# Up projection with both activation parts in one 512-column product, a shared pool of seven PSUM banks, chunked norm and block scan

## The chip, the cores and the metric

One core of a Trainium2 chip runs the program. The time is what the device reports for one execution, in microseconds (us). Engines are named as in the profile: PE (TensorE, matrix products) with PEld (its loads of the stationary operand), DVE (VectorE), ACT (ScalarE), POOL (GpSimd) and SP (the queue that issues the weight transfers).

## What is computed

Two layers of a hybrid backbone over 256 tokens of width 2048: 128 context tokens (g = 0) and 128 latent tokens (g = 1). Everything is fp32.

```python
h = modulate(x, shift1, scale1)                       # shift, scale, gate from silu(c) @ w_mod + b_mod
q, k, v, hq, hff, hfb, hi, hgt = split_in(h @ w_in)   # 2048 x 6656
att = rms_norm(attend(q, k, v, sink), attn_g)         # 8 heads
hg, s_f, s_b = hgrn_mixer(hq, hff, hfb, hi, hgt, ...) # 8 heads, forward and backward scan in chunks of 32
mix = concatenate([att, hg]) @ w_o
x = layer_norm(ALPHA * x + gate1 * mix)
ffn = square(relu(modulate(x, shift2, scale2) @ w_up)) @ w_down   # 2048 x 8192, 8192 x 2048
x = layer_norm(ALPHA * x + gate2 * ffn)
```

Within a scan of 128 tokens, a chunk's outputs take the chunk itself (`o_intra`), and the states left by the chunks before it, each decayed by the chunks between.

## The kernel before, in words

**Weights and their parts.** All weights are streamed once. An item of the main stream is a block of 512 x 512 weights: SP brings it as two raw tiles of 128 x 1024 (10 raw buffers), ACT rounds each to the high part `wh` (L1324, fp32r), and DVE takes the rest as the low part `wl` (L1325). There are four buffers for each of them, so two items. The activations are split the same way into `hh` and `hl` (`split_act`, L406). A product is then high x high + high x low + low x high: three fp32r matmuls where one would stand.

**Units.** A unit is one 512-wide output block: four items (`kg`), or fewer. In a T unit (q, hq, the two gates, and the up projection) the weight is the stationary operand: for each of 4 row blocks k and 4 column blocks m, `mm_tile` issues three matmuls of 256 columns (L436 `wh` with `hh`, L438 `wh` with `hl`, L439 `wl` with `hh`). In an N unit (k/v, hi, hgt, w_o, w_down) the activations are stationary and the weights stream, in matmuls of 512 columns (L448 to L450): rows k 0 and 1 for g = 0, then for g = 1, then rows 2 and 3 for both. Each unit accumulates in two PSUM banks of a pool of three (`accp`). When the last item is done, the unit's `done` function reads them: for the up projection `d_up` (ACT relu and square, L1214 and L1215, then `split_act` into `fh`/`fl`), for the down projection `d_down` (DVE, L1236 and L1240), for w_o `add_gated` (L887 to L892). In each of the two layers there are 16 up units, and 16 down units.

**Modulation.** Blocks of `w_mod` are dealt between the items at fixed rates (`RATE`, `PRATE`). Some go to PE (`Mod`, L203: 2-column weights at four places of the array, L223 for the first ones), the others to DVE, four multiply-adds of 128 x 1024 a block (`ModH.mac`, L266); most of those lie in the first layer's MLP.

**Tasks.** Attention, scans and norms run as generators that `pump` advances: up to two steps in the middle of an item and three at its end. Their PSUM tiles come from a pool of four banks (`sdp`, function `bank`). `scan_task` (L684; 8 a layer) computes the products within chunks (`pI`, L748), and then those across chunks into `pX` in three rounds (L777): all four heads' `kd` (128 columns) as weights, 32 columns of `qb` moving, with DVE scaling the earlier chunks between the rounds (L774), a masked copy (L794) and a last scaling (L801).

**Norms.** Both norms of a layer but the very last (`ln_last`) run as: statistics (`ln_stat`), centre and scale of eight 128 x 512 tiles on DVE (`ln_head`, L909), and `ln_mod`: per 512 features and token part four transposes on PE (L931), scale and shift (DVE L934, L936 for g = 0, ACT L940 for g = 1), and the split (L408, L409). `ln_out` then multiplies and adds the norm's gain and bias on POOL (L1002, L1003), for the residual. POOL also does part of the gated sums (L892 and L1224).

**Order.** DVE, ACT and PE instructions are ordered by a scheduler when the program is built; POOL and SP keep the order of the code. Each engine works through its own list.

## Time and profile before

| | |
|---|---|
| three runs | 2641.39, 2641.58, 2647.34 us; median 2641.58 |
| the profiled execution | 2641.68 us, of which the span from the first to the last instruction is 2639.9 |
| PE busy | 2536.6 us, 96% of the span |
| DVE, ACT, POOL busy | 1862.5, 1214.5, 230.9 us (71, 46, 9%) |
| transfers | 652.91 MB, 247 GB/s on average |
| granted TensorE clock, mean over the span | 0.988 |

A matmul's end in the profile is modelled, and matmuls overlap; what one costs in a stream is the distance from its start to the next one's. Idle time in brackets at a row's end is that of the engine just before it, with what ended it. "POOL" rows are rough.

### The profile page before, as it was taken

What the parts mean: (1) busy time and instruction counts of PE and PEld (TensorE: products, weight loads), DVE (VectorE), ACT (ScalarE), POOL (GpSimd) and SP (SyncE); (2) the same over time, 40 slices, a digit from 0 to 9 for tenths busy, and PEclk for the clock granted to TensorE, in tenths of its full rate; (3) what the DMA queues carried; (4) which work ended last, traced back from release to release, by engine and by line L of the source; (5) the groups of instructions that cost most, each with busy time, mean ns of one, the idle gap of its engine ahead of it and who ended that gap; (6) DMA issues with size and microseconds to landing.
All of it is one profiled execution on the core that took longest, in us unless ns stands there. A gap on an engine that the chain in (4) does not pass through costs nothing.

```text
span 2639.9 us, 41114 instructions
## 1 busy us (share of the span) xinstructions
PE 2536.6 (96%) x16276; PEld 2178.1 (83%) x16276; DVE 1862.5 (71%) x2290; ACT 1214.5 (46%) x1655; POOL 230.9 (9%) x266
## 2 busy tenths in 40 slices
PE   7999999998999999999999999999799999999996
PEld 4787777756988979979887989888798998998985
DVE  3455777658887777887778888877865565656656
ACT  3434554434444533534434656644454454443442
POOL 2000000014100000000014100001420000000003
PEclk9999999999999999999999999999899999999998
DMA  9889778868887878787879556566566666666663
GB/s 359 287 283 324 265 244 273 297 231 323 281 307 276 276 261 287 265 281 258 287 251 331 195 191 204 177 228 212 186 225 208 222 202 227 212 207 225 205 206 115
DMA packets 192369, 652.91 MB, mean 247 GB/s; under 512 B 22752, under 2 KB 25376, under 8 KB 192176
## 3 DMA queue, kind: packets, MB, share of 16 engines
q1 hardware_dynamic: 177680, 614.56, 68.0%
q0 software_dynamic: 11552, 33.04, 4.4%
q8 instruction: 127, 2.08, 0.3%
q10 hardware_dynamic: 2944, 2.69, 0.3%
q14 instruction: 66, 0.54, 0.1%
HBM read 643.32 MB, written 6.88 MB: 246 GB/s over the span
## 4 chain that ended last, share of the span: by engine, by line
PE 76%; DMA 10%; DVE 9%; issue 3%; ACT 1%; SPq 0%; POOL 0%; DVEq 0%; ACTq 0%; POOLq 0%
PE acc L436 12%; PE acc L439 12%; PE acc L438 12%; PE acc L448 11%; PE acc L449 11%; PE acc L450 11%; DMA raw<-in_w_mod_dram 6%; DVE wl L1325 3%; DVE ma L266 2%; PE psm L203 2%; PE pX L777 1%; DMA raw<-in_w_up_dram 1%; DMA raw<-in_w_in_dram 1%; PE psm L223 1%; DMA out_nsf_dram<-lf 1%
## 5 line engine op out<-in xcount | busy, mean ns | idle before, releaser
L1324 ACT CAST wh<-raw 128x1024 fp32r<-128x1024 f32 x784 | 821.8, 1049 | 1140.3 <-PE acc L450 489.0
L1325 DVE TENSOR_TENSOR wl<-raw,wh 128x1024 fp32r<-128x1024 f32 x784 | 971.2, 1246 | 433.3 <-ACT wh L1324 406.6
L436 PE MATMUL acc<-hh,wh 128*128 128x256 f32 x3072 | 875.9, 285 | 3.4 <-DVE q L599 1.9
L439 PE MATMUL acc<-hh,wl 128*128 128x256 f32 x3072 | 870.5, 284 | 7.9 <-DVE wl L1325 7.7
L438 PE MATMUL acc<-hl,wh 128*128 128x256 f32 x3072 | 869.7, 283 | 1.2 <-DVE hl L409 1.2
L436 PEld LDWEIGHTS acc<-hh,wh 128*128 128x128 f32 x3072 | 589.0, 192 | 39.2 <-issue 26.0
L439 PEld LDWEIGHTS acc<-hh,wl 128*128 128x128 f32 x3072 | 588.6, 192 | 11.2 <-DVE wl L1325 10.4
L438 PEld LDWEIGHTS acc<-hl,wh 128*128 128x128 f32 x3072 | 589.0, 192 | 2.9 <-DVE hl L409 2.2
L266 DVE SCALAR_TENSOR_TENSOR ma<-raw,stat,ma 128x1024 f32<-128x1024 f32 x300 | 388.5, 1313 | 113.4 <-DMA raw<-in_w_mod_dram 111.8
L448 PE MATMUL acc<-wh,fh 128*128 128x512 f32 x1024 | 401.8, 392 | 7.0 <-DVE Z L1236 6.8
L449 PE MATMUL acc<-wl,fh 128*128 128x512 f32 x1024 | 400.4, 391 | 0.4 <-DVE wl L1325 0.4
L450 PE MATMUL acc<-wh,fl 128*128 128x512 f32 x1024 | 399.7, 390 | 0.0
L448 PEld LDWEIGHTS acc<-wh,fh 128*128 128x128 f32 x1024 | 193.0, 188 | 57.8 <-DVE Z L1236 8.1
L449 PEld LDWEIGHTS acc<-wl,fh 128*128 128x128 f32 x1024 | 193.0, 188 | 40.8 <-DVE wl L1325 1.5
L450 PEld LDWEIGHTS acc<-wh,fl 128*128 128x128 f32 x1024 | 193.1, 189 | 40.4
L448 PE MATMUL acc<-wh,hh 128*128 128x512 f32 x320 | 129.5, 406 | 3.0 <-ACT hh L408 2.4
L449 PE MATMUL acc<-wl,hh 128*128 128x512 f32 x320 | 127.5, 398 | 0.3 <-DVE wl L1325 0.3
L450 PE MATMUL acc<-wh,hl 128*128 128x512 f32 x320 | 125.9, 394 | 1.9 <-DVE hl L409 1.9
L448 PE MATMUL acc<-wh,mxh 128*128 128x512 f32 x256 | 105.0, 411 | 5.9 <-DVE G L887 5.3
L876 POOL DMA_DIRECT2D G<-gr x48 | 26.3, 548 | 953.2 <-DVE Z L1241 408.9
L203 PE MATMUL psm<-raw,stat 128*2 128x512 f32 x640 | 96.6, 598 | 8.1 <-DMA raw<-in_w_mod_dram 8.1
L450 PE MATMUL acc<-wh,mxl 128*128 128x512 f32 x256 | 101.5, 398 | 0.0
(366 smaller groups left out, 2124.6 us busy)
## 6 DMA issues: line engine op xcount, KB each, us to landing
raw<-in_w_mod_dram SPq DMA_DIRECT2D x384, 512.0 KB
raw<-in_w_up_dram SPq DMA_DIRECT2D x256, 512.0 KB
raw<-in_w_down_dram SPq DMA_DIRECT2D x256, 512.0 KB
raw<-in_w_in_dram SPq DMA_DIRECT2D x208, 512.0 KB
raw<-in_w_o_dram SPq DMA_DIRECT2D x64, 512.0 KB
G<-gr POOLq DMA_DIRECT2D x48, 256.0 KB, 5.1
...
```

The source lines that it names most:

```text
L203: pe.matmul(self.ps[32 * j:32 * j + 2, :], lhsT=stat[:, k, :], rhs=raw[j // 2][:, 512 * (j % 2):512 * (j % 2) + 512], start=k == 0, stop=k ...
L223: pe.matmul(self.ps[32 * j:32 * j + 2, :], lhsT=stat[:, 4 * k + j, :], rhs=raw[j // 2][:, 512 * (j % 2):512 * (j % 2) + 512], start=k == 0 ...
L266: dve.scalar_tensor_tensor(self.acc[g], raw[h], c, self.acc[g], ALU.mult, ALU.add)
L436: pe.matmul(ps, lhsT=w0, rhs=hi[:, k], start=f and k == 0 and m % 2 == 0, stop=False, skip_group_check=True)
L438: pe.matmul(ps, lhsT=w0, rhs=lo[:, k], start=False, stop=False, skip_group_check=True)
L439: pe.matmul(ps, lhsT=w1, rhs=hi[:, k], start=False, stop=e and k == 3 and m % 2 == 1, skip_group_check=True)
L448: pe.matmul(ps, lhsT=hi[:, k, gs], rhs=wh[k], start=f and k == 0, stop=False)
L449: pe.matmul(ps, lhsT=hi[:, k, gs], rhs=wl[k], start=False, stop=False)
L450: pe.matmul(ps, lhsT=lo[:, k, gs], rhs=wh[k], start=False, stop=e and k == 3)
L777: pe.matmul(pX[:, 128 * m + 32 * c:128 * m + 32 * c + 32], lhsT=kd[:, 128 * m:128 * m + 128], rhs=qb[:, 128 * m + 32 * c:128 * m + 32 * c ...
L1324: act.copy(wh, r)
L1325: dve.tensor_tensor(wl, r, wh.bitcast(F32), ALU.subtract)
```

## The change

Six edits stand in the diff:

1. The parts of an activation that belong together lie side by side: a tile now holds two row blocks, each with 256 columns of the high part and then 256 of the low part. A new kind of unit, W, is used by the up projection: `w_tile` issues one 512-column matmul of `wh` with both parts, and one 256-column matmul of `wl` with the high part into the first half of the bank. A W unit accumulates in four banks; the second half of each holds `wh` x low alone, so `d_up` first copies it out (ACT, 128 x 256) and adds it to the first half (DVE, 128 x 256), four times a unit, and takes the relu from the sum.
2. The pools of three and four banks become one of seven.
3. In the last item of an N unit, g = 0 is finished before g = 1 begins.
4. The scan's products across chunks: two rounds of 32 x 32 (chunk 0 to 1, and 2 to 3), and one of 64 x 64, written to their own partitions of `pX`; three ACT copies take the place of the masked copy, and DVE's running products are merged.
5. The norm is centred and applied per 512 features, g = 1 first; g = 0 is scaled and shifted in four DVE instructions of 128 x 128; activation splits are in halves.
6. `ln_out`, and the sums in `add_gated` and `pre_sum`, go from POOL to DVE; `ln_out` waits 24 steps, and spreads its work.

```diff
-    accp = ctx.enter_context(tc.tile_pool(name="accp", bufs=3, space=PS))
     modp = ctx.enter_context(tc.tile_pool(name="modp", bufs=1, space=PS))
-    sdp = ctx.enter_context(tc.tile_pool(name="sdp", bufs=4, space=PS))
+    sdp = ctx.enter_context(tc.tile_pool(name="sdp", bufs=7, space=PS))
...
+        if un.kind == "N" and e:
+            for g in range(2):
+                if g == 1:
+                    between()
+                n_tile(un, g, range(4), hl, wh, wl, f, e)
+            return
...
+    def w_tile(un, m, ks, hl, wh, wl, f, e):
+
+        if f and ks[0] == 0:
+            un.ps[m] = bank("acc")
+        ps = un.ps[m]
+        for k in ks:
+            x = hl[k // 2][:, k % 2]
+            w0, w1 = (w[k][:, 128 * m:128 * m + 128] for w in (wh, wl))
+            pe.matmul(ps, lhsT=w0, rhs=x.rearrange("p a t -> p (a t)"), start=f and k == 0, stop=False,
+                      skip_group_check=True)
+            pe.matmul(ps[:, 0:256], lhsT=w1, rhs=x[:, 0], start=False, stop=e and k == 3, skip_group_check=True)
...
+        def across(ss, ts):
+            for m in range(4):
+                pe.matmul(pX[rows(ss), cols(m, ts)], lhsT=kd[:, cols(m, ss)], rhs=qb[:, cols(m, ts)],
+                          start=True, stop=True, tile_position=(0, 32 * ss.start))
+
+        across(one(c0), one(c1))
+        across(one(c2), one(c3))
...
-            for m in range(4):
-                pe.matmul(pX[:, 128 * m + 32 * c:128 * m + 32 * c + 32], lhsT=kd[:, 128 * m:128 * m + 128],
-                          rhs=qb[:, 128 * m + 32 * c:128 * m + 32 * c + 32], start=True, stop=True)
...
+        dve.tensor_tensor(kdv[:, :, c0], kdv[:, :, c0], dm[:, :, c1:c1 + 1].to_broadcast([128, 4, 32]), ALU.mult)
+        dve.tensor_tensor(qbv[:, :, c3], qbv[:, :, c3], dm[:, :, c2:c2 + 1].to_broadcast([128, 4, 32]), ALU.mult)
+        across(early, late)
+        yield
+        aTv = v3(aT, 4)
+        for ss, ts in ((one(c0), one(c1)), (one(c2), one(c3)), (early, late)):
+            act.copy(aTv[rows(ss), :, rows(ts)], v3(pX, 4)[rows(ss), :, rows(ts)])
...
-            (dve if n == 3 else pool).tensor_tensor(y, y, t, ALU.add)
+            dve.tensor_tensor(y, y, t, ALU.add)
...
+            for g in (1, 0):
+                y = yt[key, n, g]
+                dve.tensor_scalar(y, y, mr[g][0], mr[g][1], ALU.subtract, ALU.mult)
+            for g in (1, 0):
                 y = yt[key, n, g]
                 pt = bank("pt")
...
+                scale_shift(t, pt, A[:, fs], B[:, fs], g)
+                split_act(hl, 0, slice(128 * g, 128 * g + 128), v3(t, 4))
...
-                pool.tensor_tensor(y, y, gt, ALU.mult)
-                pool.tensor_tensor(y, y, bt, ALU.add)
+                dve.tensor_tensor(y, y, gt, ALU.mult)
+                dve.tensor_tensor(y, y, bt, ALU.add)
...
-                    r = u("t")
-                    act.activation(r, un.ps[b], AF.Relu)
+                    r, low = u("t"), u("e1")
+                    for j in range(2):
+                        ps, c = un.ps[2 * b + j], slice(256 * j, 256 * j + 256)
+                        act.copy(low[:, c], ps[:, 256:512])
+                        dve.tensor_tensor(r[:, c], ps[:, 0:256], low[:, c], ALU.add)
+                    act.activation(r, r, AF.Relu)
```

PE, in an up unit of the first layer, before: two row blocks k of one column block m.

```order
L436 MATMUL acc_6416<-hh_5697,wh_6395 128x256
L438 MATMUL acc_6416<-hl_5698,wh_6395 128x256
L439 MATMUL acc_6416<-hh_5697,wl_6396 128x256
L436 MATMUL acc_6416<-hh_5697,wh_6395 128x256
L438 MATMUL acc_6416<-hl_5698,wh_6395 128x256
L439 MATMUL acc_6416<-hh_5697,wl_6396 128x256
```

The same place in the changed program:

```order
L478 MATMUL acc_5819<-ha_5686,wh_5618 128x512
L480 MATMUL acc_5819<-ha_5686,wl_5619 128x256
L478 MATMUL acc_5819<-ha_5686,wh_5618 128x512
L480 MATMUL acc_5819<-ha_5686,wl_5619 128x256
L478 MATMUL acc_5824<-ha_5686,wh_5618 128x512
L480 MATMUL acc_5824<-ha_5686,wl_5619 128x256
```

The six matmuls became four (the last two rows begin the next bank), and the weight `wh` is loaded once where it was loaded twice (each matmul has a load of its own).

DVE, around the end of an up unit in the first layer, where `wl` is the next weights' low part, `ma` a modulation sum and `fl` the activation's low part; before:

```order
L1325 TENSOR_TENSOR wl_9680<-raw_9547,wh_9679 128x1024
L266 SCALAR_TENSOR_TENSOR ma_9071<-raw_9689,stat,ma_9071 128x1024
L409 TENSOR_TENSOR fl_9668<-t_9669,fh_9667 128x512
L1325 TENSOR_TENSOR wl_9684<-raw_9549,wh_9683 128x1024
L409 TENSOR_TENSOR fl_9668<-t_9674,fh_9667 128x512
L266 SCALAR_TENSOR_TENSOR ma_9072<-raw_9689,stat,ma_9072 128x1024
L1325 TENSOR_TENSOR wl_9760<-raw_9603,wh_9759 128x1024
L1325 TENSOR_TENSOR wl_9764<-raw_9605,wh_9763 128x1024
```

The same place in the changed program (`t` is the sum of both halves of a bank):

```order
L265 SCALAR_TENSOR_TENSOR ma_8700<-raw_9264,stat,ma_8700 128x1024
L1353 TENSOR_TENSOR wl_9257<-raw_9146,wh_9256 128x1024
L1242 TENSOR_TENSOR t_9236<-acc_9050,e_1705_9237 128x256
L1242 TENSOR_TENSOR t_9236<-acc_9055,e_1705_9237 128x256
L1242 TENSOR_TENSOR t_9246<-acc_9060,e_1707_9247 128x256
L265 SCALAR_TENSOR_TENSOR ma_8701<-raw_9264,stat,ma_8701 128x1024
L1242 TENSOR_TENSOR t_9246<-acc_9065,e_1707_9247 128x256
L1353 TENSOR_TENSOR wl_9261<-raw_9148,wh_9260 128x1024
L413 TENSOR_TENSOR fa_9234<-t_9236,fa_9234 128x2x256
L265 SCALAR_TENSOR_TENSOR ma_8700<-raw_9266,stat,ma_8700 128x1024
L1353 TENSOR_TENSOR wl_9323<-raw_9186,wh_9322 128x1024
L413 TENSOR_TENSOR fb_9235<-t_9246,fb_9235 128x2x256
```

Four instructions of 128 x 256 stand ahead of the activation's split, among the same work.

PE, at the first norm of the second layer, from the last matmul of w_o on, before (`pt` are the transposes; one row further down stands last):

```order
L450 MATMUL acc_17832<-wh_17817,mxl_17388 128x512
L931 MATMUL pt_17921<-ident_597,Y_17008 128x128 x4
L931 MATMUL pt_17931<-ident_597,Y_17012 128x128 x4
L931 MATMUL pt_17945<-ident_597,Y_17135 128x128 x4
L931 MATMUL pt_17955<-ident_597,Y_17139 128x128 x4
L931 MATMUL pt_17969<-ident_597,Y_17253 128x128 x4
L931 MATMUL pt_17979<-ident_597,Y_17257 128x128 x4
L931 MATMUL pt_17993<-ident_597,Y_17442 128x128 x4
L436 MATMUL acc_18035<-hh_17919,wh_17851 128x256
L436 MATMUL acc_18048<-hh_17919,wh_17851 128x256
L438 MATMUL acc_18035<-hl_17920,wh_17851 128x256
...
L931 MATMUL pt_18003<-ident_597,Y_17446 128x128 x4
```

The same place in the changed program:

```order
L468 MATMUL acc_17077<-wh_17062,mxb_16625 128x512
L967 MATMUL pt_17160<-ident_592,Y_16249 128x128 x4
L967 MATMUL pt_17174<-ident_592,Y_16245 128x128 x4
L967 MATMUL pt_17192<-ident_592,Y_16376 128x128 x4
L967 MATMUL pt_17206<-ident_592,Y_16372 128x128 x4
L967 MATMUL pt_17224<-ident_592,Y_16494 128x128 x4
L967 MATMUL pt_17238<-ident_592,Y_16490 128x128 x4
L967 MATMUL pt_17256<-ident_592,Y_16685 128x128 x4
L967 MATMUL pt_17270<-ident_592,Y_16681 128x128 x4
L478 MATMUL acc_17296<-ha_17156,wh_17096 128x512
L480 MATMUL acc_17296<-ha_17156,wl_17097 128x256
```

Before, the eighth transpose stood a dozen matmuls behind the start of the up projection; now all eight stand ahead of its first matmul.

## Rows read from the trace of the kernel before

**Rows 1.** The page: busy time of each engine, and the chain that ended last by engine.
```profile
PE 2536.6 (96%) x16276; PEld 2178.1 (83%) x16276; DVE 1862.5 (71%) x2290; ACT 1214.5 (46%) x1655; POOL 230.9 (9%) x266
...
PE 76%; DMA 10%; DVE 9%; issue 3%; ACT 1%; SPq 0%; POOL 0%; DVEq 0%; ACTq 0%; POOLq 0%
```

**Rows 2.** Busy time by stretch: PE, PEld, DVE, ACT, POOL; then clock, DMA share, GB/s.
```profile
640.00:1390.00 750.00, 738.20 (x4697) 651.63 (x4697) 598.22 (x549) 336.18 (x372) 39.13 (x35) 1.00 0.81 276
...
1900.00:2618.00 718.00, 716.40 (x4599) 654.00 (x4597) 439.31 (x395) 326.92 (x366) 45.09 (x47) 1.00 0.63 207
```

**Rows 3.** Timeline of PE: start, duration; first and last of 22 matmuls of 256 columns.
```profile
1499.77 0.28 PE L436 MATMUL acc<-hh,wh 128*128 128x256 f32 x1
...
1502.29 0.28 PE L436 MATMUL acc<-hh,wh 128*128 128x256 f32 x1
```

**Rows 4.** Timeline of PE: first and last of 37 matmuls of 512 columns.
```profile
2609.64 0.39 PE L450 MATMUL acc<-wh,fl 128*128 128x512 f32 x1
...
2617.80 0.39 PE L450 MATMUL acc<-wh,fl 128*128 128x512 f32 x1
```

**Rows 5.** Groups by line on PEld: count, busy us, mean ns | idle before.
```profile
L777 PEld LDWEIGHTS pX<-t,ed 128*128 128x128 f32 x192 | 23.6, 192 | 0.6
...
L203 PEld LDWEIGHTS psm<-raw,stat 128*2 128x2 f32 x640 | 11.2, 82 | 42.4 <-issue 20.0 <-DMA raw<-in_w_mod_dram 18.3 <-DVE w L279 0.4
...
L275 PEld LDWEIGHTS ph<-ma,ones 128*32 128x32 f32 x80 | 1.6, 108 | 2.4 <-issue 1.7
```

**Rows 6.** Timeline of PEld: eight loads of one round across chunks.
```profile
1503.19 0.97 PEld L777 LDWEIGHTS pX<-t,ed 128*128 128x128 f32 x8
```

**Rows 7.** Waits of PE for an accumulating bank: us in total, times, longest.
```profile
PE acc L448 <- DVE Z L1236: 6.8, 3, 2.4
...
PE acc L448 <- DVE G L887: 5.3, 2, 3.5
```

**Rows 8.** Timeline at one of these waits, on PE and on DVE.
```profile
939.83 0.50 PE L448 MATMUL acc<-wh,fh 128*128 128x512 f32 x1 [2.23 <-DVE Z L1236]
...
939.10 1.28 DVE L1236 TENSOR_TENSOR Z<-Z,acc 128x512 f32<-128x512 f32 x2
```

**Rows 9.** Busy time by stretch, columns as in rows 2, behind each of the five waits.
```profile
596.00:600.00 4.00, 4.00 (x14) 3.23 (x13) 3.09 (x5) 1.05 (x1) 3.18 (x4) 0.57 0.87 297
940.00:945.00 5.00, 5.00 (x16) 3.93 (x17) 2.74 (x3) 1.04 (x1) 0.00 (x0) 0.66 0.99 354
991.00:996.00 5.00, 5.00 (x17) 3.91 (x16) 4.72 (x5) 1.04 (x1) 0.00 (x0) 0.66 0.91 281
1133.00:1138.00 5.00, 2.78 (x13) 1.98 (x12) 4.19 (x5) 0.82 (x2) 2.26 (x2) 1.00 0.93 301
1868.00:1873.00 5.00, 4.33 (x12) 3.46 (x13) 4.19 (x7) 1.04 (x1) 3.54 (x4) 0.66 0.82 270
```

**Rows 10.** Timeline at the first norm of the second layer, on PE and on DVE.
```profile
1879.73 0.39 PE L450 MATMUL acc<-wh,mxl 128*128 128x512 f32 x1
1886.94 3.29 PE L931 MATMUL pt<-ident,Y 128*128 128x128 f32 x16 [6.83 <-DVE Y L909]
...
1895.97 0.75 PE L436 MATMUL acc<-hh,wh 128*128 128x256 f32 x2
...
1879.66 1.28 DVE L887 TENSOR_TENSOR G<-acc,G 128x512 f32<-128x512 f32 x2
...
1886.25 6.60 DVE L909 TENSOR_SCALAR Y<-Y,s,s 128x512 f32<-128x512 f32 x8
```

**Rows 11.** Groups by line on DVE, 640 to 1390 us.
```profile
L1325 DVE TENSOR_TENSOR wl<-raw,wh 128x1024 fp32r<-128x1024 f32 x254 | 312.3, 1241 | 59.8 <-ACT wh L1324 56.2 <-DMA raw<-in_w_up_dram 1.7 <-DMA raw<-in_w_mod_dram 1.5
L266 DVE SCALAR_TENSOR_TENSOR ma<-raw,stat,ma 128x1024 f32<-128x1024 f32 x202 | 258.9, 1300 | 78.4 <-DMA raw<-in_w_mod_dram 77.0 <-ACT ma L264 1.2
```

**Rows 12.** Groups by line on ACT and on DVE, the whole span.
```profile
L824 ACT COPY lf<-pK 128x256 f32<-128x256 f32 x16 | 6.0, 377 | 5.0 <-PE pK L815 5.0
...
L854 DVE TENSOR_TENSOR Z<-Z,Z 128x256 f32<-128x256 f32 x8 | 3.0, 419 | 0.0
```

More of the change, by code (lines that the diff above doesn't have):

```diff
@@ L152, in derive_constants @@
     def derive_constants():
[L153 removed]
+        for key in ("fi", "bi"):
             r = up.tile([128, 128], I32, tag="w", name=nm("m" + key), bufs=BUFS["w"])
@@ new lines, in mm_tile @@
+            if un.kind == "N":
+                for g in range(2):
+                    n_tile(un, g, ks, hl, wh, wl, f, e)
+                continue
+            for m in range(4):
+                if un.kind == "W":
+                    w_tile(un, m, ks, hl, wh, wl, f, e)
+                    continue
+                if f and kk == 0 and m % 2 == 0:
+                    un.ps[m // 2] = bank("acc")
+                ps = un.ps[m // 2][:, 256 * (m % 2):256 * (m % 2) + 256]
+                for k in ks:
+                    w0 = wh[k][:, 128 * m:128 * m + 128]
+                    w1 = wl[k][:, 128 * m:128 * m + 128]
+                    x = hl[k // 2][:, k % 2]
+                    pe.matmul(ps, lhsT=w0, rhs=x[:, 0], start=f and k == 0 and m % 2 == 0, stop=False,
+                              skip_group_check=True)
+                    pe.matmul(ps, lhsT=w0, rhs=x[:, 1], start=False, stop=False, skip_group_check=True)
+                    pe.matmul(ps, lhsT=w1, rhs=x[:, 0], start=False, stop=e and k == 3 and m % 2 == 1,
+                              skip_group_check=True)
@@ new lines, in n_tile @@
+    def n_tile(un, g, ks, hl, wh, wl, f, e):
+        if f and ks[0] == 0:
+            un.ps[g] = bank("acc")
+        ps = un.ps[g]
+        gs = slice(128 * g, 128 * g + 128)
+        for k in ks:
+            hi, lo = (hl[k // 2][:, k % 2, i, gs] for i in range(2))
+            pe.matmul(ps, lhsT=hi, rhs=wh[k], start=f and k == 0, stop=False)
+            pe.matmul(ps, lhsT=hi, rhs=wl[k], start=False, stop=False)
+            pe.matmul(ps, lhsT=lo, rhs=wh[k], start=False, stop=e and k == 3)
@@ new lines, in scan_task @@
+        early, late = slice(min(c0, c1), max(c0, c1) + 1), slice(min(c2, c3), max(c2, c3) + 1)
+        cols = lambda m, sl: slice(128 * m + 32 * sl.start, 128 * m + 32 * sl.stop)
+        rows = lambda sl: slice(32 * sl.start, 32 * sl.stop)
+        one = lambda c: slice(c, c + 1)
+        pX = bank("pX")
+        def across(ss, ts):
+            for m in range(4):
+                pe.matmul(pX[rows(ss), cols(m, ts)], lhsT=kd[:, cols(m, ss)], rhs=qb[:, cols(m, ts)],
+                          start=True, stop=True, tile_position=(0, 32 * ss.start))
@@ new lines, in scan_task @@
+        across(one(c0), one(c1))
+        across(one(c2), one(c3))
+        qS = lf[:, 256:512]
+        cum = small(8).rearrange("p (h c) -> p h c", h=2)
+        do = dm[:, 1::2]
+        dve.memset(cum[:, :, c0:c0 + 1], 1.0)
+        for x in range(1, 4):
+            pc, cc = order[x - 1], order[x]
+            dve.tensor_tensor(cum[:, :, cc:cc + 1], cum[:, :, pc:pc + 1], do[:, :, pc:pc + 1], ALU.mult)
+        for hl in range(2):
+            dve.tensor_tensor(qS[:, 128 * hl:128 * hl + 128].rearrange("p (c t) -> p c t", c=4),
+                              qbv[:, 2 * hl + 1], cum[:, hl, :].unsqueeze(2).to_broadcast([128, 4, 32]), ALU.mult)
@@ L920, in ln_coef, with scale_shift @@
         return A, B
+    def scale_shift(out, src, A, B, g):
+        for c in range(4):
+            o_, s_ = (x[:, 128 * c:128 * c + 128] for x in (out, src))
+            if g == 0:
+                dve.tensor_scalar(o_, s_, A[:, c, g:g + 1], B[:, c, g:g + 1], ALU.mult, ALU.add)
+            else:
+                act.activation(o_, s_, AF.Identity, scale=A[:, c, g:g + 1], bias=B[:, c, g:g + 1])
     def ln_mod(key, AB, dst):
         A, B = AB
+        mr = ln_stat(key)
         for n in range(4):
             hl = new_act("h")
-            for g in range(2):
+            fs = slice(4 * n, 4 * n + 4)
+            for g in (1, 0):
+                y = yt[key, n, g]
+                dve.tensor_scalar(y, y, mr[g][0], mr[g][1], ALU.subtract, ALU.mult)
+            for g in (1, 0):
                 y = yt[key, n, g]
```

148 lines of the change are left out of this document (41 added, 107 removed).

## The prediction

> **What bounds the kernel now.** I read the page's busy shares first: PE is busy for 96% of the span and holds 76% of the chain that ended last; DVE is at 71%, ACT at 46% [rows 1]. A busy PE need not be a working one, so the table by stretches comes next: in both MLPs PE is busy almost throughout, with a clock of 1.00, while the transfers have room (DMA share 0.81 and 0.63) [rows 2]. In the timeline of PE the matmuls then follow each other evenly: 21 steps from the first 256-column matmul to the last of 22 take 2.52 us, 120 ns each [rows 3], and 36 steps of 512 columns take 8.16 us, 227 ns each [rows 4]. So the end is set by the number and width of matmuls, plus the places where PE stands still. Changes to DVE, ACT and POOL count only where PE waits for them.
>
> The sum is made against the profiled execution: 2641.7 us with a span of 2639.9 and 1.8 around it; the median of the three runs is 2641.6, so no correction follows. A measurement of this kernel can tell about 0.3%, 8 us, from no change.
>
> **The up projection.** There are 32 up units of 4 items, each with 4 row blocks and 4 column blocks: 2048 places where three 256-column matmuls become one of 512 and one of 256. Twice 120 ns is 240, and the wide one takes 227: each place falls from 360 to 347 ns. 2048 x 13.3 ns = **27 us** saved, all on the path. The columns stay the same; what goes is the fixed part of one matmul, since a matmul's second 256 columns cost 227 - 120 = 107 ns, and its first 256 cost 120: 13 ns stand there whatever the width. Two pages differ here: the Trainium skill ("TensorE: Matmul & The Clock Gate", section "Back-to-back issue gap") gives a warm isolated matmul N/2.4 + 2.5 ns, a fixed part of 2.5 ns, by which the edit would be worth 5 us (an estimate from that page: 2048 x 2.5 ns). The rows show 13 ns in a dense stream, and the measurement decides; the rule stays as a rival.
>
> **The scan across chunks.** Before, a scan issues 24 matmuls on PE (4 heads, 3 rounds, and two instructions for each fp32 product: 384 loads over 16 scans, 192 in each of two groups like the one shown [rows 5]). Their loads start (0.97 - 0.19) / 7 = 111 ns apart [rows 6]; 16 x 24 x 111 ns = 43 us. They are bound by the load of 128 columns, not by the 32 columns that move. Loads last 192 ns for 128 columns, 108 for 32, 82 for 2 [rows 5]: 0.87 ns a column on top of some 80 that overlap. After, a scan has 16 with 32-column and 8 with 64-column weights: 28 and 56 ns by that slope, 0.9 us a scan, 14 us in all. That is 28 us less; at the old distance it would be nothing. I take **22 us**, nearer to the slope, since it gives the 111 ns of 128 columns right, and leave some for the changes between small and full products. DVE's and ACT's part of the scan lies beside PE.
>
> **The banks.** PE waits five times for the DVE that empties an accumulating bank: 6.8 us behind L1236 and 5.3 behind L887 [rows 7, 8]. Behind four of them the granted clock is 0.57 or 0.66 over 4 to 5 us [rows 9], that is 1.2 GHz for a part of it: 4 x 0.43 and three times 5 x 0.34, 6.8 us more. Together 19 us. With seven banks an N unit (two banks) finds free ones although the two before are not emptied. But W units take four: where one W unit follows another (24 places) the fourth bank of the next needs the first bank of the last. I take **14 us** saved; the ends are 0 and 19.
>
> **New work on DVE and ACT.** Each up unit gets four ACT copies (0.38 us) and four DVE additions (0.42 us) of 128 x 256 [rows 12]. ACT is at 45% in the first MLP [rows 2]. DVE had 598 of 750 us there [rows 2]; it gets 64 x 0.42 = 27 us, and 16 instructions of `ln_out` and 8 of `pre_sum` at 0.64 us (the pair of L887 takes 1.28 [rows 10]), 15 us: 640 of 736, 87% instead of 80%. What covers it is DVE's idle time: 56 us waiting for ACT's casts, 77 for modulation weights [rows 11]. Where that is gone, `wl` comes late, and PE waits. I put **4 us** on it; ends 0 and 14 (the whole gain of that layer's up units). In the second MLP DVE has 439 of 718 us [rows 2]: nothing.
>
> **The norms.** At the first norm of the second layer PE does not work on weights from 1879.73 to 1895.97 [rows 10]. The earlier finish of g = 0 brings DVE's chain forward by about one instruction of 0.64 us. Against it, all eight transposes now stand ahead of the up projection, and the last one waits for a centre instruction that has 12 scalings of 128 x 128 and 12 half splits ahead of it on DVE: 8 x 0.82 us (6.60 for eight) [rows 10], 12 x 0.42 [rows 12], and 12 at half of that, 14 us after 1886.25, or 1899 to 1900; without the slow centre pace (0.5 each) 1897. So this norm loses 1 to 4 us, and the other norms and the tail win the 0.64 us each. Net **+1 us**; ends -4 and +6.
>
> **ln_out later.** In the second layer's input projection the `Z` buffers are held until `ln_out` has stored them; ACT's two copies of the first gate unit then stand ten casts apart, and hold a bank. **+2 us**; ends 0 and 10 (two waits of the size in rows 7, with the slow clock behind).
>
> Sum: -27 - 22 - 14 + 4 + 1 + 2 = -56; 2641.7 - 56 = **2586 us**.
>
> **The rivals.**
> - *DVE sets the pace of the first MLP.* For: 87% in an ordered queue, with modulation sums that wait for transfers. Against: 133 us of its idle time stood in waits that a later DVE shortens. Price: that layer's 13.6 us and as much as 5 more: about 2604.
> - *The small matmuls across chunks keep 111 ns.* For: no matmul with 32-column weights and few moving columns stands in the trace. Against: loads shorten with their columns [rows 5]. 2586 + 22 = 2608.
> - *The wide matmul saves little,* because the fixed part belongs to something else than the count, so that 512 + 256 columns take some 358 ns. 2048 x 11 ns: 2608. Against: both distances are even over dozens of matmuls [rows 3, 4]. (This is what the page's 2.5 ns would mean.)
> - *Slower: W waits for its fourth bank.* The next W unit needs it three column blocks (6 matmul pairs of a half item, 2.08 us) after its start, and the bank got its last matmul as long before the end: DVE and ACT have 4.2 us. At rows 8 DVE released a bank when it had been done for 3.9 us (its last g = 0 matmul ended near 935.9, PE went on at 939.8). If that lag were the rule and two more us, a wait of 2.2 us and 1.7 of slow clock at 24 places cost 94 us: 2680. It decides from a lag of 4.2 us on, and turns the sign from about 2.3 us lost at each place. Against: three such lags in the first layer, none in the second.
> - *Everything comes at its good end*: -27 - 28 - 19 - 4 = -78: 2564.
>
> **How the numbers follow.** Chances: forecast 0.64 (2572 to 2598), DVE 0.13, small matmuls 0.07, wide matmul 0.02, all good 0.08, slower 0.06. The range of 8 in 10 runs from 2562 to 2613: it takes in all but the last, and leaves out two faults at once. Faster by over 0.3% (below 2633.7): 0.92; within: 0.02, taken from the forecast's share for two of the faults at once, with a little of the fourth rival; slower: 0.06, that rival beyond its point.
>
> **What would show it.** In the changed profile: pairs of 512 and 256 columns 347 ns apart in the up projection; the group of `pX` at about 14 us from start to start; no wait of the matmuls of N units for L1265 or L916 (the lines of L1236 and L887 there); DVE near 640 us in the first MLP, with `wl` waits of PE under 5 us; weights taken up again at the second layer's first norm some 16 to 20 us after the last matmul of w_o. The prediction is wrong if PE waits for `acc` at the start of W units, if DVE's idle time in the first MLP goes to nothing, or if the pairs are slower than 350 ns.

## The result, and the profile after

The changed kernel took 2600.05 us (median of four runs, 2598.75 to 2603.59), the kernel before 2641.48 beside it: 0.984 of the time, 95% interval 0.9823 to 0.9857, or 41 us less. The prediction was 2586 us with a range of 2562 to 2613: the time lies in it, and the sign is right. But 56 us were forecast, and the 15 that are missing are not one small thing: two terms were mis-sized by 12 and 6 us, and a gain that carries much of the result stood nowhere in the sum.

The profiled execution has a span of 2599.2 us (2639.9 before). Cut at the starts of the first and last matmul of each stage's weights, in us (a norm is the stretch between the last matmul of one stage and the first of the next):

| stage | before | after | difference |
|---|---|---|---|
| up to the first weights | 34.3 | 33.1 | -1.2 |
| layer 0: input projection, attention, scans, w_o | 574.0 | 564.0 | -10.0 |
| norm a | 15.1 | 17.9 | +2.8 |
| layer 0: MLP | 767.7 | 744.2 | -23.5 |
| norm b | 14.7 | 16.9 | +2.2 |
| layer 1: input projection to w_o | 473.9 | 465.8 | -8.1 |
| norm c | 16.2 | 19.0 | +2.8 |
| layer 1: MLP | 721.8 | 717.5 | -4.3 |
| tail | 22.1 | 20.8 | -1.3 |

The line of busy times, which answers to [rows 1], shows what still bounds the kernel: PE, at 96% of a shorter span. POOL lost more than half of its work.

```profile
PE 2502.0 (96%) x14228; PEld 2051.9 (79%) x14228; DVE 1895.1 (73%) x2500; ACT 1268.3 (49%) x1871; POOL 105.0 (4%) x188
```

The table by stretches (columns as in [rows 2]): both MLPs, and two stretches behind a wait of PE for a bank. DVE has 606 of 719 us in the first MLP, 84%, so it did not become the bound; in the last two rows the clock is 0.79, a part at 1.2 GHz.

```profile
640.00:1359.00 719.00, 713.18 (x3627) 585.60 (x3626) 606.46 (x619) 348.45 (x428) 11.93 (x23) 1.00 0.81 282
...
1861.00:2578.00 717.00, 714.26 (x3599) 604.01 (x3599) 461.67 (x484) 344.97 (x429) 15.64 (x30) 1.00 0.62 208
...
1218.00:1226.00 8.00, 5.92 (x27) 4.55 (x30) 7.99 (x11) 3.98 (x7) 0.00 (x0) 0.79 0.75 246
1886.00:1894.00 8.00, 5.26 (x21) 4.24 (x21) 6.49 (x9) 4.50 (x8) 0.00 (x0) 0.79 0.55 178
```

The timeline of PE in the second MLP answers to [rows 3, 4]. From the first 512-column matmul to the last one there are 14 pairs in 4.95 us: 353.6 ns a pair, where 347 were forecast.

```profile
2100.16 0.40 PE L478 MATMUL acc<-ha,wh 128*128 128x512 f32 x1
2100.39 0.28 PE L480 MATMUL acc<-ha,wl 128*128 128x256 f32 x1
...
2105.11 0.40 PE L478 MATMUL acc<-hb,wh 128*128 128x512 f32 x1
```

Averaged over the 1,985 pairs of the trace that no wait and no half clock interrupts it is 352.4: 235.5 from the wide to the narrow one and 116.9 back. The steps are uneven: in long stretches two pairs take 349 or 350 ns and the third 360 or 361. The place with three 256-column matmuls took 359.7 before, so the pair saves 7.3 ns.

What PE waits for from 33 us on, by line (us in total, times, longest); of [rows 7] nothing is left, neither L1265 nor L916 appears. In their place stand the sums of W units (L1242), the centring (L962) and the modulation copies (L229, 0.7 us in the kernel before).

```profile
PE pI L778 <- DVE e L772: 13.3, 6, 4.2
PE pt L967 <- DVE Y L962: 12.3, 3, 6.5
PE acc L478 <- DVE t L1242: 6.9, 4, 2.7
PE pt L232 <- ACT w L229: 5.6, 6, 1.9
```

The loads of the products across chunks, by line and shape (count, busy us, mean ns), answer to [rows 5]: 137 ns for 64 columns and 112 for 32, where 128 columns took 192.

```profile
L801 PEld LDWEIGHTS pX<-ed,t 128*64 128x64 f32 x64 | 4.3, 137 | 5.2 <-DVE ed L818 3.5 <-DVE wl L1353 0.7 <-DVE s L812 0.4
...
L801 PEld LDWEIGHTS pX<-t,ed 128*32 128x32 f32 x128 | 4.1, 112 | 3.0 <-issue 1.5 <-PE acc L456 0.3 <-PE acc L468 0.3
```

From start to start all matmuls of `pX` take 19.5 us, 40.0 before.

Norm c, on PE and on DVE, answers to [rows 10]. The first six centrings take 0.47 us each (0.82 before, as a mean over two kinds: see e7); then scalings and splits follow, and the last centring starts 11.3 us after the first. PE stands for it from the 24th transpose on.

```profile
1841.83 0.39 PE L468 MATMUL acc<-wh,mxb 128*128 128x512 f32 x1
1848.73 4.89 PE L967 MATMUL pt<-ident,Y 128*128 128x128 f32 x24 [6.50 <-DVE Y L962]
1859.22 1.97 PE L967 MATMUL pt<-ident,Y 128*128 128x128 f32 x8 [5.59 <-DVE Y L962]
1860.84 0.78 PE L478 MATMUL acc<-ha,wh 128*128 128x512 f32 x1
...
1848.13 2.83 DVE L962 TENSOR_SCALAR Y<-Y,s,s 128x512 f32<-128x512 f32 x6
1850.87 1.04 DVE L949 TENSOR_SCALAR ed<-pt,A,B 128x128 f32<-128x128 f32 x3
...
1859.41 0.55 DVE L962 TENSOR_SCALAR Y<-Y,s,s 128x512 f32<-128x512 f32 x1
```

DVE in the first MLP, around the wait at 1007 us: a multiply-add stands 4.3 us for its modulation weights at the head of the list, and the low part and three sums of a W unit, which have all they need, stand behind it.

```profile
1000.96 1.23 DVE L1353 TENSOR_TENSOR wl<-raw,wh 128x1024 fp32r<-128x1024 f32 x1 [0.65 <-ACT wh L1352]
1006.48 1.28 DVE L265 SCALAR_TENSOR_TENSOR ma<-raw,stat,ma 128x1024 f32<-128x1024 f32 x1 [4.30 <-DMA raw<-in_w_mod_dram]
1007.68 1.22 DVE L1353 TENSOR_TENSOR wl<-raw,wh 128x1024 fp32r<-128x1024 f32 x1
1008.82 1.08 DVE L1242 TENSOR_TENSOR t<-acc,e 128x256 f32<-128x256 f32 x3
```

### The profile page after: what moved, and what is told of

It is laid out like the page before. It is cut to its first block, busy times and chain, and to the rows that moved or that the text cites. A ratio compares the mean times of both kernels' runs of the same rounds, so it can differ in the third digit from the quotient of the medians.

```text
span 2599.2 us, 37416 instructions
## 1 busy us (share of the span) xinstructions
PE 2502.0 (96%) x14228; PEld 2051.9 (79%) x14228; DVE 1895.1 (73%) x2500; ACT 1268.3 (49%) x1871; POOL 105.0 (4%) x188
## 4 chain that ended last, share of the span: by engine, by line
PE 57%; issue 33%; DMA 5%; DVE 3%; ACT 2%; POOL 1%; SPq 0%; POOLq 0%; DVEq 0%; ACTq 0%
PE acc L478 11%; PE acc L466 8%; PE acc L468 8%; PE acc L467 8%; PE acc L480 6%; PE acc L453 3%; PE acc L455 3%; PE acc L456 3%; DMA raw<-in_w_mod_dram 2%; PE psm L202 2%; PE psm L222 1%; DMA raw<-in_w_in_dram 1%; DVE wl L1353 1%; PE pI L778 1%; DMA G<-in_lnb_dram 1%
## 5 line engine op out<-in xcount | busy, mean ns | idle before, releaser
L478 PE MATMUL acc<-ha,wh 128*128 128x512 f32 x1024 | 370.5, 401 | 6.9 <-DVE t L1242 6.9
L478 PE MATMUL acc<-hb,wh 128*128 128x512 f32 x1024 | 370.0, 401 | 0.0
L480 PE MATMUL acc<-hb,wl 128*128 128x256 f32 x1024 | 289.2, 282 | 0.0
L480 PE MATMUL acc<-ha,wl 128*128 128x256 f32 x1024 | 288.6, 282 | 0.1
L467 PE MATMUL acc<-wl,fb 128*128 128x512 f32 x512 | 199.5, 390 | 1.6 <-DVE wl L1353 1.6
L466 PE MATMUL acc<-wh,fa 128*128 128x512 f32 x512 | 200.5, 392 | 0.0
L466 PE MATMUL acc<-wh,fb 128*128 128x512 f32 x512 | 199.9, 390 | 0.0
L467 PE MATMUL acc<-wl,fa 128*128 128x512 f32 x512 | 199.5, 390 | 0.0
L468 PE MATMUL acc<-wh,fb 128*128 128x512 f32 x512 | 199.4, 390 | 0.0
L468 PE MATMUL acc<-wh,fa 128*128 128x512 f32 x512 | 199.4, 389 | 0.0
L453 PE MATMUL acc<-ha,wh 128*128 128x256 f32 x512 | 149.4, 292 | 0.0
L453 PE MATMUL acc<-hb,wh 128*128 128x256 f32 x512 | 147.6, 288 | 0.0
L455 PE MATMUL acc<-hb,wh 128*128 128x256 f32 x512 | 146.1, 285 | 0.0
L455 PE MATMUL acc<-ha,wh 128*128 128x256 f32 x512 | 145.8, 285 | 0.0
L456 PE MATMUL acc<-hb,wl 128*128 128x256 f32 x512 | 145.5, 284 | 0.0
```

Source lines behind the costliest of these rows:

```text
L453: pe.matmul(ps, lhsT=w0, rhs=x[:, 0], start=f and k == 0 and m % 2 == 0, stop=False, skip_group_check=True)
L455: pe.matmul(ps, lhsT=w0, rhs=x[:, 1], start=False, stop=False, skip_group_check=True)
L456: pe.matmul(ps, lhsT=w1, rhs=x[:, 0], start=False, stop=e and k == 3 and m % 2 == 1, skip_group_check=True)
L466: pe.matmul(ps, lhsT=hi, rhs=wh[k], start=f and k == 0, stop=False)
L467: pe.matmul(ps, lhsT=hi, rhs=wl[k], start=False, stop=False)
L468: pe.matmul(ps, lhsT=lo, rhs=wh[k], start=False, stop=e and k == 3)
```

## The experiments

Twelve kernels, in three groups of four; each group ran on one chip beside the kernel before, whose median was 2642.63, 2648.69 and 2644.97 us there. So groups are compared by their ratio to it, and 0.001 is 2.6 us. Stage times are those of the profiled execution, cut as in the table above; one execution can lie some us from the median, and where that matters it is said.

### Why a pair takes 353 ns: e1, e2, e3 and e12

In e1 the second matmul of a pair gets 512 columns as well:

```diff
-            pe.matmul(ps[:, 0:256], lhsT=w1, rhs=x[:, 0], start=False, ...)
+            pe.matmul(ps, lhsT=w1, rhs=x.rearrange("p a t -> p (a t)"), start=False, ...)
```

> The changed kernel, with the second matmul of every pair in a W unit widened to 512 columns too (low part of the weight times both parts of the activation, which adds the product low x low that the reference kernel leaves out). A pair of 512 and 256 columns takes 353.4 us/1000 = 353.4 ns on average in the changed kernel, and not 346.7 (120 + 226.7). Theory A, alternating widths cost it: a stream of 512 columns alone runs at 226.7 ns, a pair at 453, 2048 x 100 ns = +204 us, 2804 us. Theory B, the form of W units costs it (every matmul brings other weights than the one before, the activation's two parts are read as one row): some 230 ns each, a pair at 460, +218 us, 2818 us.

2805.81 us (one run). On the timeline of PE, 24 matmuls lie between the two rows: 5.44 us, 227 ns each.

```profile
2030.25 0.39 PE L478 MATMUL acc<-hb,wh 128*128 128x512 f32 x1
...
2035.69 0.39 PE L478 MATMUL acc<-ha,wh 128*128 128x512 f32 x1
```

Averaged, a pair takes 453.6. So a W unit's form costs nothing: other weights for every matmul, activation parts read as one row and four banks run at the 227 ns of [rows 4]. What costs 5.7 ns a pair (352.4 against 120 + 226.7) is that 512 and 256 columns stand in one stream.

In e2 the order within a column block is 512, 512, 256, 256:

```diff
         for k in ks:
             x = hl[k // 2][:, k % 2]
...
-            pe.matmul(ps[:, 0:256], lhsT=w1, rhs=x[:, 0], start=False, ...)
+        for k in ks:
+            x = hl[k // 2][:, k % 2]
+            pe.matmul(ps[:, 0:256], lhsT=wl[k][:, 128 * m:128 * m + 128], rhs=x[:, 0], start=False, ...)
```

> The changed kernel, with the two rows of a W unit's column block in the order 512, 512, 256, 256 instead of 512, 256, 512, 256: same matmuls, half as many changes of width. Theory A (a change of width costs some 3.4 ns): two pairs take 700 instead of 707 ns, 1024 x 6.7 ns = 7 us less, 2593 us. Theory B (the form of W units): no change of the distances, 2600 us but for waits for the low part, which is needed 227 ns later: at most 2 us less.

2590.56 us, 0.9801 (0.9784 to 0.9818). Rows of PE, two matmuls each; 12 pairs from the first to the last row in 4.18 us, 348.3 ns a pair:

```profile
2100.33 0.63 PE L477 MATMUL acc<-ha,wh 128*128 128x512 f32 x2
2100.79 0.40 PE L481 MATMUL acc<-ha,wl 128*128 128x256 f32 x2
...
2104.51 0.63 PE L477 MATMUL acc<-hb,wh 128*128 128x512 f32 x2
```

As expected of theory A, and about 10 us less for a swap of two lines: averaged, a pair takes 348.3 ns, and 2048 x 4.1 ns are 8.4.

e12 went on: two column blocks together, four matmuls of 512 and then four of 256 (on top of e11, below).

```diff
+                for m in (0, 2):
+                    w_tile(un, (m, m + 1), ks, hl, wh, wl, f, e)
...
+        for m in ms:
...
+            for k in ks:
+                x = hl[k // 2][:, k % 2]
+                pe.matmul(un.ps[m], lhsT=wh[k][:, 128 * m:128 * m + 128], ...
...
+        for m in ms:
+            for k in ks:
+                x = hl[k // 2][:, k % 2]
+                pe.matmul(un.ps[m][:, 0:256], lhsT=wl[k][:, 128 * m:128 * m + 128], rhs=x[:, 0], start=False, ...
```

> The kernel of e11, with two column blocks of a W unit together: four matmuls of 512 columns, then four of 256. A quarter of the changes of width of the changed kernel instead of half: 3.4 ns a pair less if a change of width costs 3.4 ns, divided by two for the half that is left, 512 x 6.7 ns = 3.5 us less than e11. Rival: the fourth bank is needed 0.47 us earlier, and waits come back: no gain.

2587.29 us, 0.9781 (0.9759 to 0.9803), where e11 has 0.9763: no gain, and not for want of banks. The pairs themselves are slower, 12 in 4.21 us or 351 ns:

```profile
2100.55 1.09 PE L477 MATMUL acc<-hb,wh 128*128 128x512 f32 x4
...
2104.76 1.09 PE L477 MATMUL acc<-hb,wh 128*128 128x512 f32 x4
```

So "a change of width costs 3.4 ns" falls: half the changes gave 4.1 ns a pair back, a quarter of them only 1.7 (350.7 averaged). Nor does the cost stand at the changes: in e2 a wide matmul comes 233 ns before the next one whether that is wide or narrow (227 in e1), and a narrow one 115 or 116 (120 among its like). That mixing costs is shown; by what, these runs leave open.

e3 puts the up projection back into T units and keeps all else.

```diff
-                put_unit(Unit("W", lambda kg, nb=4 * sc + i: a["w_up"][l, nb, kg], ...
+                put_unit(Unit("T", lambda kg, nb=4 * sc + i: a["w_up"][l, nb, kg], ...
...
-                        act.copy(low[:, c], ps[:, 256:512])
-                        dve.tensor_tensor(r[:, c], ps[:, 0:256], low[:, c], ALU.add)
-                    act.activation(r, r, AF.Relu)
+                    act.activation(r, un.ps[b], AF.Relu)
```

> The changed kernel with the up projection back in T units (three 256-column matmuls, two banks, ACT's relu straight from PSUM), all other edits kept. Theory 'pair at 353': the up projection's matmuls take 2048 x (360 - 353.4) = 13.5 us more, and the waits for the sums of W units (some 7 us, and 3 to 5 us of half clock behind them) go: 2602 to 2606 us. Rival 'the wide matmul is worth the forecast 27 us and something else took it back': 2617 us or more.

2619.76 us, 0.9913 (0.9897 to 0.993): the rival's number, but not its reason. In the profiled execution the MLPs take 754.1 and 719.7 us, 9.9 and 2.2 more than with W units. In the second the pairs are worth 1024 x 7.3 ns = 7.5; less the 2.7 us of waits at W units' starts and 1.7 of half clock, 3.1 would be left, near the 2.2. In the first, PE waits 6.7 us for low parts that the changed kernel waits 1.6 for. W units are worth 16 to 19 us here, of which 15 are the pairs.

### The norms: e4

```diff
         for n in range(4):
-            hl = new_act("h")
-            fs = slice(4 * n, 4 * n + 4)
             for g in (1, 0):
                 y = yt[key, n, g]
                 dve.tensor_scalar(y, y, mr[g][0], mr[g][1], ALU.subtract, ALU.mult)
+        for n in range(4):
+            hl = new_act("h")
+            fs = slice(4 * n, 4 * n + 4)
```

> The changed kernel with the centring of all eight 128 x 512 tiles ahead of the first scaling in each norm, in place of two tiles per 512 features. Theory 'the last centring stands behind scalings and splits of DVE': the three norms between matmuls of weights shorten from 17.9, 16.9 and 19.0 us to 13 to 16 each, 6 to 11 us less in all, 2589 to 2594 us. Rival 'the banks decide': the eight transposes hold seven banks, and the up projection's four wait for them; the norms stay within 1.5 us of what they are, 2597 to 2601 us.

2598.75 us, 0.9839 (0.982 to 0.9859). On PE at norm c all 32 transposes run in one go, and weights are taken up 12.3 us after the last matmul of w_o:

```profile
1841.10 0.39 PE L468 MATMUL acc<-wh,mxb 128*128 128x512 f32 x1
1847.94 5.66 PE L968 MATMUL pt<-ident,Y 128*128 128x128 f32 x32 [6.45 <-DVE Y L960]
1853.41 0.50 PE L478 MATMUL acc<-ha,wh 128*128 128x512 f32 x1
```

The norms fall to 12.7, 13.3 and 12.3 us, 15.5 less in all: more than expected, and seven banks do not hold them up. But the time hardly moves. In the profiled execution, the fastest of the four, the span is 6.8 us shorter, in the median of the runs nothing is left; the first MLP takes 4.8 us more and the input projections 3.3, and in that MLP PE waits for low parts (7.1 us in 8 waits at N units, against 1.6):

```profile
PE acc L467 <- DVE wl L1354: 7.1, 8, 2.2
```

The cause in the norms is shown. Of where their gain went the profile shows about half, in these stages; the rest lies between the profiled execution and the median and is not shown, and neither is why low parts come later there than in the changed kernel.

### The banks: e5 and e9

e5 is the kernel before with the two pools merged; e9 adds edit 3.

```diff
-    accp = ctx.enter_context(tc.tile_pool(name="accp", bufs=3, space=PS))
-    sdp = ctx.enter_context(tc.tile_pool(name="sdp", bufs=4, space=PS))
+    sdp = ctx.enter_context(tc.tile_pool(name="sdp", bufs=7, space=PS))
...
-                        un.ps[g] = accp.tile([128, 512], F32, tag="acc", name=nm("acc"))
+                        un.ps[g] = bank("acc")
```

```diff
+        if un.kind == "N" and e:
+            for g in range(2):
+                if g == 1:
+                    between()
+                n_tile(un, g, range(4), hi, lo, wh, wl, f, e)
+            return
```

> The kernel before with its pools of three and four PSUM banks made one of seven, nothing else. Theory 'the bank term as forecast': the waits behind L1236 and L887 and the half clock behind them go, 12 to 19 us less: 2623 to 2630 us, and the first layer's MLP falls from 767.7 to 755 to 758 us. Rival 'scans and norms take the banks, and waits for them come instead': 2635 us or more.

> The kernel before with one pool of seven banks, and with g = 0 finished before g = 1 in the last item of an N unit (edits 2 and 3). Seven banks alone gave 1.005 of the time before. Theory 'the bank term needs the order too': the first layer's MLP falls from 760.6 us to about 754 (what it was with all edits but W units), the loss in the input projections stays; 0.999 to 1.003 of the time before. Rival 'the order does nothing': as seven banks alone, 1.004 to 1.006.

e5: 2659.43 us, 1.005 (1.0026 to 1.0074), **slower**. e9: 2652.76 us, 1.0029 (1.0014 to 1.0044). So the rival of e5 holds, and e9 lies where its first theory had it. In the first MLP the term is there: 760.6 and 757.2 us instead of 767.7, with no wait behind `d_down` left. But most other stages that take banks lost: the input projections with the scans took 578.9 and 481.5 us in e5 (574.0 and 473.9 before), 578.0 and 479.3 in e9, norm c 18.9 and 20.6 (16.2), the second MLP 3 us more in both. Waits of PE in e9:

```profile
PE pt L939 <- DVE Y L917: 12.0, 3, 10.8
...
PE pt L232 <- ACT w L229: 4.4, 6, 0.7
```

The second row grew from 0.7 us, and is the same 4.4 in e5 with the pool alone, so that row of the changed kernel comes from there. A pool is shared: with it the order of PE's list changed for the tasks too, and they wait in more places for their data. That the scheduler places them earlier because a bank can be had is how I read it; it was not tried by itself.

### The scan: e6

The kernel before with edit 4 alone (its lines stand in the change above).

```diff
-                pe.matmul(pX[:, 128 * m + 32 * c:128 * m + 32 * c + 32], lhsT=kd[:, 128 * m:128 * m + 128], ...
+                pe.matmul(pX[rows(ss), cols(m, ts)], lhsT=kd[:, cols(m, ss)], rhs=qb[:, cols(m, ts)], ...
```

> The kernel before with the new products across chunks alone (edit 4). Theory 'the shorter matmuls come off the path in full': 40.0 us of pX fall to 19 or 20, and the time by as much: 2619 to 2623 us. Rival 'the longer chain of one scan (merged products on DVE, three copies on ACT ahead of pO) makes PE wait': 6 to 10 us of it come back, 2626 to 2632 us.

2637.48 us, 0.9959 (0.9941 to 0.9977), 6 to 16 us less. The matmuls across chunks take 20.0 us from start to start, 40.0 before: the price was right. That half of it does not reach the end is the rival's size, but its wait is small: PE stands 12.7 us for `pI`, as before (12.8), and 3.6 more at `pX` and `pO`. The execution that was profiled is the slowest of the ten (2645.12 us), so its stages show where the gain can be lost and not what the edit is worth. The input projection of layer 0 shows its share (564.9 us, -9.1); that of layer 1 takes 473.4, as before, and the MLPs take 7.9 and 4.2 us more. In the input projection of layer 1 the mean clock (third column from the end) is 0.97, where the kernel before has 1.00 between 1406 and 1864 us:

```profile
1406.00:1879.00 473.00, 456.74 (x3001) 404.10 (x3000) 370.73 (x557) 268.86 (x457) 59.09 (x74) 0.97 0.67 217
```

Some 24 of the 473 us are at half clock, which costs 12, more than the scans' share of 10. The two longest of these stretches follow waits of PE of 3 us each for the scan's DVE work (at 1528 and 1671 us). Between kernels this stage has 3 to 24 us at half clock, with no order that these runs explain, and e10, with the old scan, has 17; so the lost half is not shown to be the new scan's doing.

### The sums on DVE: e7 and e10

e7 is the changed kernel with the sums of edit 6 on POOL again (the diff; the same for `add_gated` and `pre_sum`); e10 is the kernel before with the opposite edit.

```diff
-                dve.tensor_tensor(y, y, gt, ALU.mult)
-                dve.tensor_tensor(y, y, bt, ALU.add)
+                pool.tensor_tensor(y, y, gt, ALU.mult)
+                pool.tensor_tensor(y, y, bt, ALU.add)
```

> The changed kernel with ln_out's two operations, the sum in add_gated and the product in pre_sum back on POOL (edit 6 without its engine change). Theory 'DVE's load is a small cost': DVE has some 15 us less in the first layer's MLP, and that stage falls by 0 to 4 us; the whole 2594 to 2600 us. Rival 'DVE's load is what the in-projection of the second layer and the norms lost': 5 to 9 us less there, 2590 to 2594 us. Third: a later POOL sum delays the norms' statistics, 2602 us or more.

> The kernel before with ln_out, the sum in add_gated and the product in pre_sum on DVE instead of POOL, nothing else (ln_out without its delays). Theory 'POOL's sums slow DVE': the eight centrings at the second layer's first norm take 0.5 to 0.55 us each and not 0.82, and that norm falls from 16.2 to 13.5 or 14.5 us; against it ln_out's waits for its gain and bias rows stand in DVE's list at the start of each MLP. Sum -6 to +2 us, 0.998 to 1.001. Rival 'as forecast, load alone': the norms stay as long as they were, and the first layer's MLP takes 4 us more: 1.0015 or more.

e7: 2630.24 us, 0.993 (0.9907 to 0.9953), some **24 us slower** than the changed kernel. e10: 2633.9 us, 0.9953 (0.9935 to 0.9971), 12 us faster than before. The theories of a small cost fall, e7's first two and the rival of e10. What e10's first theory said of the centrings holds (at twice its best price), and what e7's third said of a delay ahead of the norms. In e7 norms a and c take 23.8 and 29.0 us, 15.9 more than in the changed kernel. Its timeline at norm c, on DVE and then on POOL:

```profile
1862.31 0.69 DVE L916 TENSOR_TENSOR G<-acc,G 128x512 f32<-128x512 f32 x1 [1.68 <-DMA G<-gr]
...
1876.28 0.40 DVE L949 TENSOR_SCALAR ed<-pt,A,B 128x128 f32<-128x128 f32 x1
1876.60 1.16 DVE L413 TENSOR_TENSOR ha<-ed,ha 128x256 fp32r<-128x256 f32 x1
...
1879.41 0.41 DVE L413 TENSOR_TENSOR ha<-ed,ha 128x256 fp32r<-128x256 f32 x1
...
1884.10 1.48 DVE L962 TENSOR_SCALAR Y<-Y,s,s 128x512 f32<-128x512 f32 x1
...
1855.44 2.20 POOL L921 TENSOR_TENSOR Y<-Y,G 128x512 f32<-128x512 f32 x1 [1.40 <-DVE G L916]
1857.59 1.09 POOL L905 DMA_DIRECT2D G<-gr  x2
...
1876.02 1.46 POOL L1033 TENSOR_TENSOR Y<-Y,G 128x512 f32<-128x512 f32 x1
...
1878.83 0.58 POOL L1027 DMA_DIRECT2D G<-in_lng_dram  x1
...
1883.97 1.32 POOL L1034 TENSOR_TENSOR Y<-Y,G 128x512 f32<-128x512 f32 x1
```

While POOL works on a sum, DVE's split takes 1.16 us; while POOL only issues a transfer, 0.41. The centring takes 1.48 instead of 0.55. The scaling from PSUM (L949) keeps its 0.40 beside the same sum. These slow instructions end 0.28 and 0.29 us after the sum beside them (1877.76 against 1877.48, 1885.58 against 1885.29), so they look like ones that wait for its end rather than run at a slower pace; these ends are all that shows it. The Trainium skill ("GPSIMD Engine Reference", section "Key points") says that POOL shares its SBUF interfaces with VectorE, and names DVE instructions with two SBUF inputs or in a 2-port mode as the ones that contend. The split has two such inputs, and its rows agree, at about three times its duration; in which mode the centring runs, no row shows.

The first row of DVE and the first two of POOL are a second path. POOL issues the transfer of the gate's rows (`gr`, L905) only behind a gated sum (L921), and DVE stands for it; the first centring then starts 10.4 us after the last matmul of w_o, where it takes 6.3 in the changed kernel. So of the 10.0 us that norm c is longer, 4.1 are lost ahead of the first centring and 5.9 behind it, beside the sums; in norm a it is 2.1 and 3.7.

The sums beside DVE were also the "slow centre pace" of [rows 10]: in the kernel before, POOL ran `ln_out` at that moment. Of the eight centrings the five ahead of it take 0.46 us from start to start, and the three beside it 1.44 each, with the mean of 0.82 that the prediction used:

```profile
1888.12 1.64 POOL L1002 TENSOR_TENSOR Y<-Y,G 128x512 f32<-128x512 f32 x1 [5.14 <-PE pt L931]
1889.83 1.33 POOL L1003 TENSOR_TENSOR Y<-Y,G 128x512 f32<-128x512 f32 x1
...
1888.53 4.31 DVE L909 TENSOR_SCALAR Y<-Y,s,s 128x512 f32<-128x512 f32 x3
```

In e10 the same eight centrings take 3.74 us instead of 6.60, and norm c 12.8 instead of 16.2:

```profile
1880.93 3.74 DVE L909 TENSOR_SCALAR Y<-Y,s,s 128x512 f32<-128x512 f32 x8
```

Over the whole trace DVE's instructions beside a sum of POOL take 57 us more in the kernel before than the same ones elsewhere, 47 in e7, and 5 in the changed kernel and in e10; not all of it is on PE's path. That it makes the norms longer is shown. The norms are 4.2 of the 10.1 us by which e10's profiled execution is shorter, and 16.9 of e7's 24.2 with both paths; for the rest, in which stages move both ways, the cause is not shown.

### Both orders, and banks emptied by ACT: e8 and e11

e8 is the changed kernel with the edits of e2 and e4 together.

> The changed kernel with both orders turned: 512, 512, 256, 256 in W units, and all eight centrings first in each norm. If the two gains are independent: the profile's span falls by 14 us (2599.2 to 2585.2) and 6.8 us (to 2592.4), together 2578 us of span, some 2582 us of time. Rival: with the norms shorter, ln_out and modulation press on DVE in the first layer's MLP (749.0 us there against 744.2), and low parts that come late take back the order's gain: 2587 us or more.

e8: 2587.55 us, 0.9767 (0.9748 to 0.9786), better than the change (0.984) and than e2 (0.9801). The gains add up in part, as the rival had it. Its longest wait left in an MLP, 5.6 us, stands at the start of a W unit, 53 us into the second MLP. There DVE's list stands at the bias row of `ln_out` (L1037), and three sums that free banks come behind it:

```profile
1897.22 0.69 DVE L1037 TENSOR_TENSOR Y<-Y,G 128x512 f32<-128x512 f32 x1 [3.45 <-DMA G<-in_lnb_dram]
1897.84 1.22 DVE L1356 TENSOR_TENSOR wl<-raw,wh 128x1024 fp32r<-128x1024 f32 x1
1898.97 1.08 DVE L1245 TENSOR_TENSOR t<-acc,e 128x256 f32<-128x256 f32 x3
```

e11 frees the banks without DVE:

```diff
-                        act.copy(low[:, c], ps[:, 256:512])
-                        dve.tensor_tensor(r[:, c], ps[:, 0:256], low[:, c], ALU.add)
+                        act.copy(both, un.ps[2 * b + j])
+                        dve.tensor_tensor(r[:, 256 * j:256 * j + 256], both[:, 0:256], both[:, 256:512], ALU.add)
```

> The kernel of e8 (both orders turned), with ACT copying both halves of a W unit's bank (128 x 512) to SBUF and DVE adding there, so that a bank comes free without DVE. Theory 'PE's waits at the start of a W unit come from DVE's list standing at a transfer (modulation weights, or ln_out's rows)': those waits (5.8, 2.2 and 1.8 us in e8) and the half clock behind them (6.8 us of it) go, 8 to 14 us less than e8: 0.971 to 0.974 of the time before. Rival 'ACT becomes late': the casts of weights wait behind the longer copies (0.63 instead of 0.37 us), gain under 4 us or a loss.

2584.92 us, 0.9763 (0.9741 to 0.9784): no difference to e8 that can be told. The mechanism is right: no wait of PE for these sums is left, and the second MLP falls from 715.3 to 710.2 us. But the first rises from 742.4 to 747.6. From 600 us on, PE waits 13.5 us for low parts against 7.5 in e8. The row of e8, and then the two of e11:

```profile
PE acc L467 <- DVE wl L1356: 7.5, 7, 3.6
```

```profile
PE acc L467 <- DVE wl L1356: 9.7, 9, 3.6
...
PE acc L481 <- DVE wl L1356: 3.8, 6, 1.7
```

## Why the prediction was right, and where it was not

- **The bound** held: PE's matmuls and its waits set the end, and DVE at 84 to 85% of the first MLP did not.
- **The up projection, -27 us: measured -15** (2048 x 7.3 ns). The step that failed is "twice 120 ns is 240, and the wide one takes 227": both distances were read in streams of one width, and added up for a stream of two. e1 shows that each is right where it was read, e2 and e12 that the mixture costs 1.6 to 5.7 ns a pair, by its order. The rival of a matmul that saves little was half true; its reason, the fixed part, was not the one. By the N/2.4 + 2.5 ns that the Trainium skill ("TensorE: Matmul & The Clock Gate", section "Back-to-back issue gap") gives for a warm isolated matmul, a pair would take 325 ns (an estimate from that page). No stream in these runs comes near it.
- **The scan, -22: measured -20.6** on PE's path (40.0 to 19.5; the text had 43 to 14 by the slope, and took 22 of it); e6 shows that some half of it need not reach the end.
- **The banks, -14:** the waits named are gone, and in the first MLP e5 and e9 give 7 and 10 us for it. That a pool is shared by everybody was left out, and this costs more than it gives when it is done alone. The fourth rival's wait came too, at 4 of 24 places (6.9 us of waits, and two half-clock stretches of 3.4 us). Its lag of DVE was not a steady one: DVE stood at a transfer, in the rows at 1006.48 for modulation weights.
- **DVE's load, +4:** no such cost as load. But the price was looked for on the wrong side. The 64 sums and 24 other instructions were counted as work that DVE gets, and nothing for the work that POOL no longer does, beside DVE and ahead of its own transfers. e7 puts 24 us on it within the change, e10 12 us alone: without it the change would have been at 0.993, some 2623 us and outside the range.
- **The norms, +1: measured +6.5** (+7.8 in the three norms, -1.3 in the tail). For norm c the text had the mechanism and its size (1 to 4 us; 2.8 measured, weights taken up 19.0 us after w_o, 16 to 20 foretold). It then let the other two win 0.64 us each, though they run through the same code; they lost 2.8 and 2.2. The last centring behind scalings and splits, which e4 shows to be the cause, was in the text, and was priced for one norm of three. With the sums on POOL, in e7, the norms are 16.9 us longer still.
- **ln_out, +2:** the waits that it was put down for did not come: PE waits for no accumulating bank in the second layer's input projection. PE's waits for `pI`, 13.3 us, are what they were (12.8, on two lines). The input projections gave 18.1 us less in all, of which the shorter `pX` alone is 20.6. What took the rest back is not settled; modulation copies (5.6 instead of 0.7 us) and half clock are parts of it.

Two of the prediction's own signs of being wrong came true, PE's waits for `acc` at the start of W units and pairs slower than 350 ns. So the range held with errors on both sides: some 18 us too much from pairs and norms, and a gain from POOL that the sum did not have. That they partly cancel is luck; the bound and the scan's price are not. How the rest of the sum divides between banks, waits at W units and the input projections, no run settles.
